# Modulation projections of a four-layer decoder step: eight single units in a row of weight units become bursts of four, and two of them move to another place in the plan

## The chip, the cores and the metric

The kernel runs on one NeuronCore of a Trainium2 chip. The metric is device time in microseconds (us) of one execution; the median of three runs before the change is 1632.8 us (1631.33 to 1634.27).

## What is computed

Four trunk layers run over 288 token rows at once: 256 rows of one prompt and 8 samples of 4 rows. Everything is fp32, with D = 1024. Each layer has two sub-layers, a token mixer and a squared-ReLU MLP, and each sub-layer is modulated per sequence (adaLN):

```
mod = silu(c) @ w_ada[i] + b_ada[i]            # 9 sequences, 1024 -> 6 x 1024
sh1, sc1, g1, sh2, sc2, g2 = split(mod, 6)
h = x * (1 + sc1) + sh1
x = layer_norm(ALPHA * x + g1 * mixer(h), ...)  # 0: gMLP, 1: HGRN2, 2: MLA, 3: gMLP
h = x * (1 + sc2) + sh2
x = layer_norm(ALPHA * x + g2 * (square(relu(h @ w1)) @ w2), ...)
```

The mixers are: layers 0 and 3 a chunked gating MLP (gMLP), layer 1 a gated linear recurrence with state (HGRN2), layer 2 a latent attention over a paged cache of 2048 positions (MLA). `w_ada` is a 1024 x 6144 matrix per layer, 24 MB, and it is read once for nine rows of input.

## The kernel before

Activations are kept transposed: features on partitions, the 288 rows along the free dimension. A weight matrix comes in **weight units** of 1 MB (1024 rows x 256 columns). A unit is loaded into a `raw` tile, split into a rounded high part (`hi`, ScalarE, L240) and the rest (`lo`, VectorE, L241), each in two pieces, and is then used in 16 positions of three matmuls each (`mm3`, L294, L295, L297: hi x hi, lo part x hi, hi x lo part), 48 matmuls of 128x128 by 288 columns. There are 5 `raw` tiles (`RAWB`) and 3 pairs of `hi` and `lo` (`HLB`), so at most three units are split ahead.

A **modulation unit** is 1 MB of `w_ada`, loaded into the same 5 `raw` tiles but used as it is, in fp32: `ada_step` (L492 on, its matmul is L504) issues four matmuls of 512 columns, one for each group of 32 output partitions, and the profile shows them as 8 instructions. An `ada` unit covers 128 rows of two of the six chunks (eight units make chunks 0 and 1, or 2 and 3); an `adh` unit covers 256 rows of one chunk (four units make chunk 4, the second scale, or chunk 5, the second gate). After the last unit of a chunk `ada_end` or `adh_end` copies the sums out, turns them with small matmuls (L539 or L525) and writes them to `modT`. A layer needs 8 + 8 + 4 + 4 units. There are 88 of them behind the first two chunks of layer 0, which have a form of their own (L558).

**The order of loads** is written out by hand: `run` makes one `plan`, a list of weight and modulation units, and `load_next` issues its loads in that order on SyncE's queue (L138 for modulation, L145 for weights). `advance` issues a load whenever fewer than five units from the first unfinished one on have been issued, splits a weight unit if a `hi`/`lo` pair is free (`pump`), and otherwise tries `ada_step`. So a modulation unit that isn't used yet holds one of the five tiles.

**When a modulation unit may be used** is set by `s.quota` (how many may go), `s.alim` (up to which unit of the plan), `s.hold`, and `s.fence` (an instruction that they stand behind on TensorE). `wfree` is called at the last matmul of each weight unit; it raises the quota by one and moves the fence to that matmul, so one modulation unit follows each weight unit. At each LayerNorm boundary (`run`) the quota is set to `FILL` = 4 and the fence to the last matmul of the statistics, so four units run in the LayerNorm, where TensorE waits for the normalized rows. `ada_need` forces all units up to a key, whatever the quota.

The framework (Tile) schedules instructions by priority in program order: an instruction may be placed on its engine ahead of earlier ones that aren't ready in the scheduler's model. On the chip each engine then keeps the order that the scheduler chose. `issue_after` fixes one instruction behind another.

In the plan before, `spread` puts four modulation units behind the first two weight units of a stage and then one behind each weight unit (mixers) or every second one (MLP). A mixer of layers 1 to 3 takes chunks 2 and 3 (eight units, four of which run in the LayerNorm ahead of it) and chunk 4; an MLP takes chunk 5 (in the LayerNorm ahead of it) and the next layer's chunks 0 and 1. `before_out` stands ahead of the mixer's output projection (four weight units, here called o0 to o3), `before_end` ahead of the MLP's last matrix. The output projection's first two units run interleaved over their eight k tiles, so that the k tiles that are ready first go first.

In the HGRN2 mixer four pairs of heads follow one another; the last pair's chain of small matmuls, VectorE and ScalarE steps has no weight units behind it but the output projection. In the MLA mixer the paged cache rows also go through the `raw` tiles, two per sample; the merge of the partial softmaxes and the value projection stand ahead of `before_out`.

Of the kernel before, what the change touches and what calls it, by code (L numbers as in the profile page):

```python
# [45 lines left out]
R2 = (1, 5)  # L46
# [3 lines left out]
AHEAD = 4  # L50

FILL = 4
SPACE = (1, 1, 1)

VEC = {}

# [1 line left out]
class Net:  # L58
# [42 lines left out]
    def set_plan(s, plan):  # L101
        s.plan = plan
        s.idx = {}
        w = 0
        s.wlist = []
        s.alist = []
        s.ndone = 0
        s.fence = None
        s.hold = True

        s.quota = 99
        s.alim = -1
        s.quiet = False
        s.rs_ins = s.rs_act = None
        for n, (kind, key, src) in enumerate(plan):
            assert key not in s.idx, key
            s.idx[key] = n
            if kind in ("w", "w2", "t", "q"):
                s.wlist.append(n)
            if kind == "a":  # L120
                s.alist.append(n)
        s.rawt = {}
        s.done = [False] * len(plan)
        s.nd = 0
        s.freed = 0
        s.nsplit = 0
        s.piece = 0
        s.wdone = 0
        s.hl = {}
# [132 lines left out]
    def wfree(s, key):  # L262
        assert s.wlist[s.wdone] == s.idx[key], (key, s.plan[s.wlist[s.wdone]][1])
        s.wdone += 1
        del s.hl[key]
        s.quota = max(s.quota, 0) + 1
        s.fence = s.last_mm
        s.advance()


# [1424 lines left out]
            out.append(u)  # L1695
        return out + a

    def spread(s, w, a, first, n, step):

        out, a = list(w[:first]) + list(a[:n]), list(a[n:])  # L1700
        for k, u in enumerate(w[first:]):
            out.append(u)
            if a and k % step == step - 1:
                out.append(a.pop(0))
        return out + a

    def before_out(s, i):
        if i != s.layers[0]:
            s.ada_need(("adh", i, 4, 3))
        s.hold = True  # L1710

    def before_end(s, i):
# [7 lines left out]
    def run(s):  # L1720
        L = s.layers
        af = s.ada_first_units(L[0])
        plan = []
        for n, i in enumerate(L):
            kind = i % 3
            a, o = getattr(s, ("plan_gmlp", "plan_hgrn", "plan_mla")[kind])(i)
            f = s.plan_ffn(i)
            first, last = n == 0, n + 1 == len(L)
            sc2, g2 = s.adh_units(i, 4), s.adh_units(i, 5)
            if first:  # L1730
                plan += af[:4] + a[:2] + af[4:] + s.merge(a[2:] + o, s.ada_units(i, 1) + sc2, *FIRST)
            else:
                plan += s.spread(a, s.ada_units(i, 1) + sc2, 2, FILL, SPACE[i % 3]) + o
            fill = g2 + ([] if last else s.ada_units(L[n + 1], 0))
            plan += s.spread(f[0] + f[1], fill, 2, FILL, 2) + f[2] + f[3]
        s.set_plan(plan)
        s.alim = s.idx[("adh", L[0], 4, 3)]
        s.setup()
        s.late_setup()
        for n, i in enumerate(L):  # L1740
            first, last = n == 0, n + 1 == len(L)
            s.hold = False
            s.alim = s.idx[("adh", i, 4, 3)]
            if n:
                s.quota = FILL
                s.advance()
            s.rs_ins = None
            getattr(s, ("gmlp", "hgrn", "mla")[i % 3])(i)
            if first:
                s.ada_need(("adh", i, 4, 3))  # L1750
            s.prep_ab(i, 1, s.lnv(0, i), s.lnv(1, i))
            if first:
                s.bias_means()
            s.boundary(1, i)
            s.fence = s.last_stat
            s.hold, s.quota = False, FILL
            s.alim = s.idx[("adh", i, 5, 3) if last else ("ada", L[n + 1], 0, 7)]
            s.advance()
            s.ada_need(("adh", i, 5, 3))
            s.quota = 0  # L1760
            s.rs_ins = None
            s.ffn(i)
            if not last:
                s.boundary(0, i)
                s.fence = s.last_stat
            else:
                s.store_y(i)
# [89 lines left out]
```

## Time and profile before

| | |
|---|---|
| median of three runs | 1632.8 us |
| the profiled execution's own time | 1632.95 us |
| its span (first to last instruction) | 1631.2 us |
| TensorE matmul busy | 1580.3 us, 97% |
| VectorE busy | 1026.6 us, 63% |
| ScalarE busy | 801.4 us, 49% |
| granted TensorE clock, mean | 0.989 of full speed |
| read from HBM | 324.09 MB, 203 GB/s over the span |

The profile is one execution. PE is TensorE's matmuls and PEld its weight loads, DVE is VectorE, ACT ScalarE, SP SyncE, whose queue issues the loads. An instruction's line is that of the kernel's source; tiles are named as `out<-in`. Matmuls are pipelined: two neighbours of 288 columns start 0.13 us apart though each lasts 0.29 us, so costs on TensorE are read from start to start.

### The profile page before, as it was taken

To read this page: it belongs to the slowest core of one execution; us is meant where nothing else is said; L and a number is where in the kernel's file an instruction comes from. 1 tells how busy PE (TensorE), PEld (TensorE's weight loads), DVE (VectorE), ACT (ScalarE), POOL (GpSimd) and SP (SyncE) were. 2 spreads that over 40 slices of the span, in tenths; PEclk is the share of its full clock that TensorE was granted. 3 is DMA by queue.
4 is the path that set the end of the run, shared out by engine and by line. 5 is a ranking of instruction groups with operands and counts; after the bars stand their busy time and mean duration, and the time that the engine had idled before them with its cause. 6 is when DMAs were issued, how large, how long until landed. Compare 5 with 4: busy or idle time off the path is not lost.

```text
span 1631.2 us, 30568 instructions
## 1 busy us (share of the span) xinstructions
PE 1580.3 (97%) x12538; PEld 1402.3 (86%) x12538; DVE 1026.6 (63%) x2290; ACT 801.4 (49%) x1437; POOL 53.2 (3%) x70
## 2 busy tenths in 40 slices
PE   7999999999999989999999999999999999999997
PEld 3878889998789878999977666878999888899997
DVE  3558745658768886556686335595455685874655
ACT  2554633545767755335353445364354463653542
POOL 1000000000110100000002120000000000000000
PEclk9998999999999999999999999899999999999999
DMA  9976876458764567755476445287654676655531
GB/s 323 340 254 209 297 239 181 157 179 269 230 190 158 158 200 273 245 166 170 157 256 248 143 151 207 95 278 261 217 174 158 236 263 200 207 182 170 166 104 43
DMA packets 222719, 332.61 MB, mean 204 GB/s; under 512 B 7171, under 2 KB 196041, under 8 KB 213362
## 3 DMA queue, kind: packets, MB, share of 16 engines
q1 hardware_dynamic: 215954, 299.86, 55.7%
q0 software_dynamic: 6624, 30.78, 5.6%
q8 instruction: 99, 1.62, 0.4%
q14 instruction: 42, 0.34, 0.1%
HBM read 324.09 MB, written 6.53 MB: 203 GB/s over the span
## 4 chain that ended last, share of the span: by engine, by line
PE 87%; DVE 6%; DMA 3%; ACT 2%; issue 1%; SPq 0%; POOL 0%; DVEq 0%; ACTq 0%; POOLq 0%
PE mm L294 23%; PE mm L297 22%; PE mm L295 22%; PE ada L504 4%; DMA raw<-in_w_ada 2%; PE mm L1456 1%; DVE lo L241 1%; PE mx L1474 1%; PE mm L1510 1%; PE mx L1528 1%; PE ada L558 1%; PE mx L863 1%; PE mx L965 1%; PE mx L1478 1%; PE mm L1556 1%
## 5 line engine op out<-in xcount | busy, mean ns | idle before, releaser
L241 DVE TENSOR_TENSOR lo<-raw,hi 128x1024 fp32r<-128x1024 f32 x360 | 434.4, 1222 | 172.1 <-ACT hi L240 172.0
L240 ACT ACTIVATE hi<-raw 128x1024 fp32r<-128x1024 f32 x360 | 371.0, 1052 | 262.1 <-PE mm L297 198.5
L294 PE MATMUL mm<-Hi,hi 128*128 128x288 f32 x1064 | 317.4, 302 | 7.6 <-ACT Hi L1209 4.5
L295 PE MATMUL mm<-Hi,lo 128*128 128x288 f32 x1064 | 314.4, 299 | 0.1
L297 PE MATMUL mm<-FL,hi 128*128 128x288 f32 x1024 | 303.6, 296 | 0.0
L294 PE MATMUL mm<-FH,hi 128*128 128x288 f32 x1024 | 303.3, 296 | 0.0
L295 PE MATMUL mm<-FH,lo 128*128 128x288 f32 x1024 | 299.2, 292 | 0.0
L297 PE MATMUL mm<-Lo,hi 128*128 128x288 f32 x1064 | 297.4, 298 | 0.0
L294 PEld LDWEIGHTS mm<-Hi,hi 128*128 128x128 f32 x1064 | 200.2, 188 | 36.2 <-issue 11.7
L294 PE MATMUL mm<-OH,hi 128*128 128x288 f32 x704 | 207.1, 298 | 1.4 <-ACT OH L705 1.3
L295 PEld LDWEIGHTS mm<-Hi,lo 128*128 128x128 f32 x1064 | 200.6, 189 | 7.2 <-issue 5.0
L295 PE MATMUL mm<-OH,lo 128*128 128x288 f32 x704 | 205.7, 296 | 0.5 <-DVE lo L241 0.5
L297 PEld LDWEIGHTS mm<-Lo,hi 128*128 128x128 f32 x1064 | 193.8, 189 | 8.6 <-issue 7.5
L295 PEld LDWEIGHTS mm<-FH,lo 128*128 128x128 f32 x1024 | 195.1, 191 | 2.5 <-issue 2.5
L294 PEld LDWEIGHTS mm<-FH,hi 128*128 128x128 f32 x1024 | 192.4, 188 | 5.0 <-issue 5.0
L297 PE MATMUL mm<-OL,hi 128*128 128x288 f32 x704 | 195.1, 296 | 0.0
L297 PEld LDWEIGHTS mm<-FL,hi 128*128 128x128 f32 x1024 | 191.9, 187 | 0.0
L784 ACT ACTIVATE r<-mm 128x288 f32<-128x288 f32 x128 | 52.3, 412 | 184.5 <-PE mm L297 179.0
L294 PEld LDWEIGHTS mm<-OH,hi 128*128 128x128 f32 x704 | 132.1, 188 | 11.9 <-issue 5.0
L295 PEld LDWEIGHTS mm<-OH,lo 128*128 128x128 f32 x704 | 132.4, 188 | 0.8 <-DVE lo L241 0.7
L297 PEld LDWEIGHTS mm<-OL,hi 128*128 128x128 f32 x704 | 128.0, 188 | 1.9 <-issue 1.7
L786 DVE TENSOR_TENSOR s<-r 128x288 f32<-128x288 f32 x128 | 58.2, 457 | 110.7 <-ACT r L784 110.7
(434 smaller groups left out, 2067.3 us busy)
## 6 DMA issues: line engine op xcount, KB each, us to landing
raw<-in_ffn_w SPq DMA_DIRECT2D x128, 1024.0 KB, 5.6
raw<-in_w_ada SPq DMA_DIRECT2D x88, 1024.0 KB, 5.5
raw<-in_a_w_in SPq DMA_DIRECT2D x16, 1024.0 KB, 7.3
raw<-in_b_w_in SPq DMA_DIRECT2D x16, 1024.0 KB, 6.6
raw<-in_w_ada SPq DMA_DIRECT2D x16, 512.0 KB, 9.8
raw<-in_a_w_out SPq DMA_DIRECT2D x8, 1024.0 KB, 6.6
St<-in_state_hgrn POOLq DMA_DIRECT2D x8, 512.0 KB, 5.6
out_hs_s<-St POOLq DMA_DIRECT2D x8, 512.0 KB, 3.8
```

The costliest lines, as they stand in the source:

```text
L240: nc.scalar.activation(hi[:, a:b], r[:, a:b], AF.Copy)
L241: nc.vector.tensor_tensor(lo[:, a:b], r[:, a:b], hi[:, a:b].bitcast(F32), op=OP.subtract)
L294: mm(out, w[0], x[0], start=first, stop=False)
L295: mm(out, w[1], x[0], start=False, stop=False)
L297: s.last_mm = mm(out, w[0], x[1], start=False, stop=last).ins
L504: nc.tensor.matmul(s.pa[32 * j:32 * j + 32, :], x, w, start=(k == 0), stop=(k == last), skip_group_check=True)
L558: mm = nc.tensor.matmul(pa[r0:r0 + 32, :], s.scT[:, 2 * kp + par, :], t[:, par, h, :], start=(kp == 0), stop=(kp == 3), skip_group_check=True)
L784: nc.scalar.activation(r, ps[:, :T], AF.Relu)
L786: nc.vector.tensor_tensor(sq, r, r, op=OP.mult)
L863: nc.tensor.matmul(pt[:, 128 * q:128 * q + 128], vt01[:, q, sl], s.wsT[:, c, :], start=True, stop=True)
L965: mm(pt[32 * b:32 * b + 32, 64 * hh + 32 * g:64 * hh + 32 * g + 32], k[:, hh, a:a + 32], q[:, hh, a:a + 32], start=True, stop=True, skip_g ...
L1456: tr(pt[:, 128 * n:128 * n + 128], lat[b][t // 8][:, t % 8, 128 * c:128 * c + 128], s.id)
```

## The change

A stage's modulation units outside the LayerNorms get their quota not after every weight unit but at two points, behind the stage's second and fourth weight unit (`wburst`), four at a time; the plan is reordered to it (`burst`). The mixer's limit `alim` ends with chunks 2 and 3, and chunks 4 and 5 (second scale, second gate) are planned among o0 to o3 and forced in `before_out`: both chunks in layers 1 and 2, there without a fence, chunk 4 alone in layer 3. So the MLPs of layers 1 and 2 no longer take chunk 5, and their LayerNorm runs the next layer's first four units in its place. In layer 0 the mixer's plan stays as it is, but its units get no fence; its MLP still takes chunk 5 in the LayerNorm and then has all eight units of the next layer outside it.

```diff
-SPACE = (1, 1, 1)
...
+        s.wburst = ()
...
         del s.hl[key]
-        s.quota = max(s.quota, 0) + 1
-        s.fence = s.last_mm
+        if s.wdone in s.wburst:
+            s.quota, s.fence = FILL, s.last_mm
         s.advance()
...
-    def spread(s, w, a, first, n, step):
...
+    def burst(s, w, a):
+        return list(w[:2]) + list(a[:FILL]) + list(w[2:3]) + list(a[FILL:]) + list(w[3:])

     def before_out(s, i):
         if i != s.layers[0]:
+            s.ada_need(("ada", i, 1, 7))
+            if i % 3:
+                s.fence = None
             s.ada_need(("adh", i, 4, 3))
+            if i != s.layers[-1]:
+                s.ada_need(("adh", i, 5, 3))
         s.hold = True
...
-                plan += s.spread(a, s.ada_units(i, 1) + sc2, 2, FILL, SPACE[i % 3]) + o
-            fill = g2 + ([] if last else s.ada_units(L[n + 1], 0))
-            plan += s.spread(f[0] + f[1], fill, 2, FILL, 2) + f[2] + f[3]
+                plan += s.burst(a, s.ada_units(i, 1)) + s.merge(o, sc2 + ([] if last else g2), *R2)
+            fill = (g2 if first or last else []) + ([] if last else s.ada_units(L[n + 1], 0))
+            plan += s.burst(f[0] + f[1], fill) + f[2] + f[3]
...
-            s.alim = s.idx[("adh", i, 4, 3)]
+            s.alim = s.idx[("ada", i, 1, 7) if n else ("adh", i, 4, 3)]
             if n:
                 s.quota = FILL
+                s.wburst = (s.wdone + 2, s.wdone + 4)
                 s.advance()
...
-            if first:
-                s.ada_need(("adh", i, 4, 3))
+            s.ada_need(("adh", i, 4, 3))
...
             s.alim = s.idx[("adh", i, 5, 3) if last else ("ada", L[n + 1], 0, 7)]
+            s.wburst = (s.wdone + 2, s.wdone + 4)
             s.advance()
             s.ada_need(("adh", i, 5, 3))
-            s.quota = 0
```

`R2` is (1, 5): `merge` puts o0 first, then five modulation units, then o1, then the rest, then o2 and o3.

## Rows read from the trace of the kernel before

**Rows 1.** The page: busy time by engine, shares of the chain that ended last

```profile
PE 1580.3 (97%) x12538; PEld 1402.3 (86%) x12538; DVE 1026.6 (63%) x2290; ACT 801.4 (49%) x1437; POOL 53.2 (3%) x70
...
PE 87%; DVE 6%; DMA 3%; ACT 2%; issue 1%; SPq 0%; POOL 0%; DVEq 0%; ACTq 0%; POOLq 0%
```

**Rows 2.** Windows, modulation matmuls alone: stretch, length, busy (count), clock, DMA share, GB/s

```profile
45.00:156.50 111.50, 13.82 (x96) 0.95 0.76 263
160.80:377.40 216.60, 8.53 (x64) 1.00 0.64 209
```

**Rows 3.** Timeline of PE around one single unit in layer 0's MLP

```profile
208.80 0.30 PE L294 MATMUL mm<-Hi,hi 128*128 128x288 f32 x1
208.94 0.29 PE L295 MATMUL mm<-Hi,lo 128*128 128x288 f32 x1
209.16 1.06 PE L504 MATMUL ada<-raw,scT 128*32 128x512 f32 x8
210.15 0.40 PE L297 MATMUL mm<-Lo,hi 128*128 128x288 f32 x1
210.39 0.29 PE L294 MATMUL mm<-Hi,hi 128*128 128x288 f32 x1
```

**Rows 4.** Timeline of PEld at the same place: the first weight load behind the unit

```profile
210.15 0.19 PEld L297 LDWEIGHTS mm<-Lo,hi 128*128 128x128 f32 x1 [0.84 <-issue]
```

**Rows 5.** Timeline of PE in the LayerNorm ahead of layer 0's MLP

```profile
156.57 3.64 PE L504 MATMUL ada<-raw,scT 128*32 128x512 f32 x32
160.84 0.40 PE L294 MATMUL mm<-Hi,hi 128*128 128x288 f32 x1 [0.63 <-ACT Hi L705]
```

**Rows 6.** Waits of PE over the whole span: waiter, releaser, us in total, times, longest

```profile
PE ada L504 <- DMA raw<-in_w_ada: 2.0, 4, 0.7
```

**Rows 7.** Issues on SP's queue around layer 0's first LayerNorm

```profile
153.15 4.91 SPq L145 DMA_DIRECT2D raw<-in_ffn_w  x2
158.55 0.35 SPq L138 DMA_DIRECT2D raw<-in_w_ada  x1
159.41 3.28 SPq L145 DMA_DIRECT2D raw<-in_ffn_w  x2
172.76 0.34 SPq L138 DMA_DIRECT2D raw<-in_w_ada  x1
```

**Rows 8.** Issue to landing (last number, us): the load at 160.27, the one at 172.76

```profile
raw<-in_ffn_w SPq DMA_DIRECT2D x1, 1024.0 KB, 13.2
...
raw<-in_w_ada SPq DMA_DIRECT2D x1, 1024.0 KB, 5.2
```

**Rows 9.** The page's costliest groups: the two halves of a split; busy, mean ns

```profile
L241 DVE TENSOR_TENSOR lo<-raw,hi 128x1024 fp32r<-128x1024 f32 x360 | 434.4, 1222 | 172.1 <-ACT hi L240 172.0
L240 ACT ACTIVATE hi<-raw 128x1024 fp32r<-128x1024 f32 x360 | 371.0, 1052 | 262.1 <-PE mm L297 198.5
```

**Rows 10.** Groups of PE by line: the small matmuls behind a chunk of four units

```profile
L525 PE MATMUL mx<-con,adas 128*128 128x18 f32 x64 | 8.7, 271 | 0.0
```

**Rows 11.** Windows, PE alone, ahead of the output projections of layers 1 and 2

```profile
570.50:575.00 4.50, 0.00 (x0) 1.00 0.72 209
575.00:579.00 4.00, 3.98 (x18) 0.57 0.00 0
1015.00:1025.00 10.00, 5.27 (x49) 1.00 0.96 299
1025.00:1036.60 11.60, 10.76 (x52) 0.56 0.20 78
```

**Rows 12.** Waits of PE from 548 to 580, the end of the HGRN2 mixer

```profile
PE mm L294 <- ACT Hi L1209: 4.5, 1, 4.5
PE mx L1038 <- DVE k L991: 1.3, 1, 1.3
PE mx L1030 <- DVE k L991: 0.9, 1, 0.9
```

**Rows 13.** Issues on SP's queue from 499 to 552, layer 1

```profile
532.55 13.55 SPq L145 DMA_DIRECT2D raw<-in_ffn_w  x2
```

More of the change, by code (lines that the diff above doesn't have):

```diff
@@ L1696, in merge @@
         return out + a
-    def spread(s, w, a, first, n, step):
[L1700 to L1705, printed above, removed]
+    def burst(s, w, a):
+        return list(w[:2]) + list(a[:FILL]) + list(w[2:3]) + list(a[FILL:]) + list(w[3:])
     def before_out(s, i):
         if i != s.layers[0]:
+            s.ada_need(("ada", i, 1, 7))
+            if i % 3:
+                s.fence = None
             s.ada_need(("adh", i, 4, 3))
+            if i != s.layers[-1]:
+                s.ada_need(("adh", i, 5, 3))
         s.hold = True
```

## The prediction

> **What bounds the kernel now.** The page first: PE is busy in 97% of the span and holds 87% of the chain that ended last [rows 1]. So a change is worth what it takes from PE's stream, or what it adds to it in waits. Next the windows cut at the LayerNorms, counting the modulation matmuls alone [rows 2]: 64 instructions, that is 8 units, stand outside the LayerNorms in layer 0's MLP and as many in five more stages (MLPs of layers 1 and 2, mixers of layers 1, 2, 3), and 96 in layer 0's mixer. Then what one costs. Around a single unit [rows 3] the matmul before it starts at 208.94 and the second one after it at 210.39, 1.45 us for what takes two steps of 0.133 (208.80 to 208.94 is one): **1.19 us for a single unit**. Four in a row last 3.64 us [rows 5] where one lasts 1.06, so each further unit adds (3.64 - 1.06)/3 = **0.86 us**. A burst of four costs 1.19 + 3 x 0.86 = 3.77, against 4.76 for four singles. The LayerNorm's four are free: after them PE still waits 0.63 us for the rows [rows 5].
>
> Where do the 0.33 us of a single unit go? The weight load of the first ordinary matmul behind it starts together with that matmul, at 210.15, after 0.84 us without any load [rows 4]. The Trainium skill ("TensorE: Matmul & The Clock Gate", section "Step-by-step: what each phase is for") says that PE pulls weight loads ahead of matmuls in flight. By that, a single unit would cost its own 0.86 and grouping nothing; the eight bursts below would give 8 us less, 1625.5 us in place of my 1617.5. The skill's "TensorEngine Tiling (Array Packing)", "Key Properties", says instead that a change of tiling mode drains the engine, and the 0.84 us agree with that. I go by the row.
>
> **The change, part by part** (against the profiled execution's own 1632.95 us; the median is 0.15 less, so one sum serves both).
>
> *MLPs of layers 1 and 2.* Before: 8 singles, 9.5 us. After: four of them are in the LayerNorm, in the place of the second gate, and four in one burst, 3.8. Saved 5.7 each. Their waits for loads go too: 2.0 us in four waits in the whole kernel [rows 6], all in the three MLPs, of which I count half here and half for layer 0. Is everything there in time? The plan has four units and one weight unit (f3) behind the split of f2. In layer 0 the load that waits for f2's split goes out at 172.76, 12 us after the first matmul (160.84 [rows 5, 7]), and lands 5.2 us later [rows 8]. Here that load is f3: it lands at 17, its first half is split 2.3 us later (1.05 + 1.22 [rows 9]), and it is wanted after two weight units (96 steps, 12.8), the burst (3.8) and f2 (6.4), at 23. Spare: 3.5 us. Nothing is added. **Saved 12.4.**
>
> *Mixers of layers 1 and 2, the first part.* Before: 8 singles outside the LayerNorm; after: one burst of four there, and the other four go to the next part. **Saved 11.4** for both.
>
> *Mixer of layer 3.* 8 singles become two bursts, the second ahead of the projection, behind an old fence. o0, its four units and o1 fit the five tiles, since o0 gives its tile back when it is split. **Saved 2.0.**
>
> *MLP of layer 0.* 8 singles become two bursts: 9.5 + 1.0 of the waits - 7.5 = 3.0 saved. But here the plan has all eight between f2 and f3. Four sit in tiles until the first burst at 173.9. Their tiles come free about 175.1, 175.9, 176.8 and 177.6, and three more modulation loads go out ahead of f3. In the trace the fourth of four loads issued within 2.6 us, the one at 160.27, landed 13.2 us after its issue [rows 7, 8]. So f3 lands at 190.8, its first half is split at 193.1, and f2 is done at 173.9 + 3.8 + 6.4 = 184.1: **a wait of 9.0 us**. Alone in the queue it would take 5.2, a wait of 1.0; I take the fourth-of-four, which is the same situation. A wait like that also has a price behind it. After the 4.5 us without matmuls at 570.5 the granted clock was 0.57 for 4.0 us, with 18 matmuls where full speed (2.4 GHz) would need 2.4 us [rows 11]: 1.6 us. So this stage **loses 7.6**. On PE the second burst and f4 stand behind f3's matmuls, on SP's queue the loads of f4 and on stand behind f3's. What is late next would be f4: its load can take f3's tile once f3 is split (195), and lands at 200.4, before the second burst ends at about 205. If it has to wait for a unit of that burst instead, it comes some 4 us late; I keep that for the range.
>
> *The eight units ahead of the projection, layers 1 and 2.* Eight units in about three groups are 8 x 0.86 + 3 x 0.33 = 7.9 us, and two chunk ends (8 small matmuls each, 8.7/8 = 1.1 [rows 10]) 2.2, together 10.1 of PE work; the 2.2 disappear elsewhere. What can hide it in layer 1: waits of 4.5, 1.3 and 0.9 us [rows 12], now partly covered by the projection's ready k tiles; and the slow 4.0 us behind them, worth 1.6 if the clock stays up [rows 11]. 10.1 - 2.2 - 6.7 - 1.6 is about 0. In layer 2, PE has 4.7 us idle from 1015 to 1025, then 11.6 us at a clock of 0.56 [rows 11], worth up to 5 at full speed, of which I count half: again about 0. Loads: in layer 1 the two loads behind the projection's four now go out from 532.6 to 546 [rows 13]; in the new plan o0 and five modulation units are first, so those five sit in the five tiles by about 551, while o1 and three more units wait for the first five to run. These have no fence, so the first time PE lacks ready work, about 549, they go; o1 then lands about 555. Bounds for a layer: 3 us gained if the waits swallow all and the clock holds; 8 lost (7.9) if nothing hides. I take **1.5 lost each**, nearer to full cover: a unit can hold up a small matmul of the chain by its 0.86, once or twice. On DVE and ACT the splits of o1 to o3 come later than now (2.3 us a half, in turn [rows 9]); the chain's own steps have priority over them.
>
> *Layer 0's mixer.* Same units in the same plan, without a fence; they ran as singles at the pace of their loads (DMA share 0.76 [rows 2]). Nothing, within 2 us either way.
>
> Sum: 12.4 + 11.4 + 2.0 - 7.6 - 3.0 = 15.2 saved; 1632.95 - 15.2 is 1617.8, 1617.6 against the median. I say **1617.5**.
>
> **The rivals.**
>
> *Everything hides* (1606): f3's load passes quickly and the tails swallow their units and hold the clock. For it: DMA share 0.20 from 1025 [rows 11]. Against it: the queue is in order. 6 of the 9 us back, and 2 x 3 us gained rather than 3 lost: 1632.8 - 27.
>
> *Grouping does not pay* (1625.5): the scheduler places ready ordinary matmuls between the units of a burst, or the drain is overlapped as above. Against it: all four-unit groups in LayerNorms stayed whole, but there nothing else was ready.
>
> *The projection's second weight unit comes late* (slower, 1645). It is loaded behind five modulation units that hold all tiles. If the scheduler leaves those until the last wait at 570.5, o1 and the last three units go out from 571.5 to 574, the last lands 13.2 us later, 587 in place of a start at 575, and the three units (2.6) stand ahead of the projection: some 15 us in layer 1 and likewise in layer 2. 18.2 saved without the tails, less 30: 12 slower. It decides if the first forced unit of layer 1 starts after about 562; in one layer alone it gives about 1630. For it: no wait on PE is long before 549. Against it: they have no fence, and PE already reached for projection work at 548.
>
> **How the numbers follow.** Forecast 0.62; everything hides 0.12; grouping does not pay 0.11; late unit in both layers 0.10, in one layer (about no change) 0.05. A measurement tells 0.2% (3.3 us) from no change. The first three lie below 1629.5: faster 0.85, same 0.05, slower 0.10. The range reaches down past the case in which all hides, by the 2 us of layer 0's mixer (1604), and up past the unpaid case and a second wait in layer 0, to 1631.
>
> **What would show it.** Right: L504 groups of 32 instructions outside the LayerNorms, lasting 3.6 us; one at about 173.9 followed by 48 matmuls and a wait of about 9 us for a load or split; in layers 1 and 2 about 40 fewer single-unit steps, and both MLP windows 6 us shorter; the 4.5 us gap of layer 1's end mostly filled. Wrong: groups broken up by other matmuls, waits of the first projection matmuls on `hi` or `lo`, or MLP windows of layers 1 and 2 that don't shrink.

## The result, and the profile after

The changed kernel takes 1614.75 us (median; 1609.68 to 1621.26) against 1632.64 of the kernel before on the same chip: a ratio of 0.9892, with a 95% interval of 0.9855 to 0.9930. That is 17.9 us less, where 15.2 were forecast. The profiled execution took 1613.43 us, its span is 1611.7, 19.5 less than before's. The head of the page (busy time, chain) against [rows 1]:

```profile
PE 1566.9 (97%) x12538; PEld 1399.0 (87%) x12538; DVE 1025.4 (64%) x2290; ACT 798.8 (50%) x1435; POOL 53.1 (3%) x70
...
PE 87%; DVE 6%; DMA 4%; ACT 2%; issue 1%; SPq 0%; POOL 0%; DVEq 0%; ACTq 0%; POOLq 0%
```

TensorE has the same number of instructions and is still the bound. Of the 19.5 us, 13.4 are busy time and the rest is idle time. Where they went is read from windows cut at the last matmul of each LayerNorm's statistics (L642). Columns: stretch, length, PE busy (count), granted clock, DMA share, GB/s. Before, in order: MLP 0 (of layer 0), mixer and MLP 1, mixer and MLP 2:

```profile
155.90:379.10 223.20, 221.60 (x1656) 1.00 0.65 210
379.10:596.00 216.90, 206.71 (x2229) 0.99 0.61 193
596.00:818.00 222.00, 220.97 (x1653) 1.00 0.65 213
818.00:1069.90 251.90, 241.30 (x2058) 0.98 0.53 183
1069.90:1292.60 222.70, 221.06 (x1653) 1.00 0.65 213
```

The kernel after, with mixer 0 as its first line:

```profile
93.40:151.90 58.50, 57.34 (x389) 0.97 0.65 214
151.90:380.70 228.80, 221.61 (x1656) 0.99 0.63 205
380.70:592.30 211.60, 207.37 (x2270) 1.00 0.66 218
592.30:807.80 215.50, 214.41 (x1614) 1.00 0.61 200
807.80:1060.20 252.40, 246.81 (x2098) 0.99 0.56 199
1060.20:1275.50 215.30, 214.36 (x1614) 1.00 0.62 201
```

All stages against before and the forecast's terms (lengths from the cuts themselves, which the windows round to 0.1 us; mixer 3 in two parts, about its inner LayerNorm):

| stage | before, us | after, us | difference | forecast |
|---|---|---|---|---|
| start and mixer 0 | 94.6 + 61.3 | 93.4 + 58.5 | -4.0 | 0 |
| MLP 0 | 223.1 | 228.8 | +5.7 | +7.6 |
| mixer 1 | 217.0 | 211.6 | -5.4 | -4.2 |
| MLP 1 | 222.0 | 215.5 | -6.5 | -6.2 |
| mixer 2 | 251.9 | 252.4 | +0.5 | -4.2 |
| MLP 2 | 222.7 | 215.3 | -7.4 | -6.2 |
| mixer 3 | 40.3 + 72.3 | 39.1 + 71.1 | -2.4 | -2.0 |
| MLP 3 and end | 226.0 | 226.0 | 0 | 0 |

Of the terms that were forecast every sign but one came, and mixer 2 gave nothing. Now one row group per mechanism. First, a burst in layer 0's MLP on PE's timeline (start, us, instruction):

```profile
170.46 0.29 PE L297 MATMUL mm<-Lo,hi 128*128 128x288 f32 x1
170.68 3.64 PE L504 MATMUL ada<-raw,scT 128*32 128x512 f32 x32
174.25 0.40 PE L294 MATMUL mm<-Hi,hi 128*128 128x288 f32 x1
174.49 0.29 PE L295 MATMUL mm<-Hi,lo 128*128 128x288 f32 x1
```

From 170.46 to 174.49 are 4.03 us for what takes two steps of 0.133: the burst costs 3.76, as worked out (3.77). Second, what follows it: waits of PE in layer 0's MLP (waiter, releaser, total, times, longest), SP's issues there, and windows of PE.

```profile
PE mm L294 <- ACT hi L240: 6.2, 1, 6.2
PE mm L295 <- DVE lo L241: 0.4, 1, 0.4
```

```profile
153.66 20.19 SPq L138 DMA_DIRECT2D raw<-in_w_ada  x8
174.38 28.57 SPq L145 DMA_DIRECT2D raw<-in_ffn_w  x6
```

```profile
180.00:185.00 5.00, 0.90 (x7) 0.97 0.82 291
185.00:190.00 5.00, 2.54 (x9) 0.50 0.01 2
190.00:195.00 5.00, 5.00 (x34) 0.85 0.70 210
```

Eight modulation loads stand ahead of f3 on the queue, f3 goes out at 174.38, and the `hi` of its first half is there at 187.0, 6.2 us after f2's matmuls are done. The granted clock falls to its lower level (0.50) in this wait and is up again at about 191. Third, the ends of the mixers of layers 1 and 2, from L1017 of the last pair of heads and from the last L1608 to the LayerNorm's first matmul L639. Before:

```profile
549.20:593.70 44.50, 36.80 (x271) 0.96 0.38 124
1030.90:1067.60 36.70, 34.89 (x243) 0.93 0.23 76
```

After:

```profile
540.90:590.00 49.10, 47.17 (x357) 1.00 0.78 276
1010.00:1057.90 47.90, 46.12 (x298) 0.93 0.66 235
```

In layer 1 PE's waits in this stretch fall from 7.7 us (length less busy) to 1.9, the wait of 4.5 [rows 12] to 1.0, and the clock stays up. In layer 2 nothing comes back: the stretch is 11.2 us longer.

### The profile page after: what moved, and what is told of

It is laid out like the page before. It is cut to its first block, busy times and chain, and to the rows that moved or that the text cites. A ratio compares the mean times of both kernels' runs of the same rounds, so it can differ in the third digit from the quotient of the medians.

```text
span 1611.7 us, 30562 instructions
## 1 busy us (share of the span) xinstructions
PE 1566.9 (97%) x12538; PEld 1399.0 (87%) x12538; DVE 1025.4 (64%) x2290; ACT 798.8 (50%) x1435; POOL 53.1 (3%) x70
## 4 chain that ended last, share of the span: by engine, by line
PE 87%; DVE 6%; DMA 4%; ACT 2%; issue 1%; SPq 0%; POOL 0%; DVEq 0%; ACTq 0%; POOLq 0%
PE mm L294 23%; PE mm L297 23%; PE mm L295 22%; PE ada L504 3%; PE mm L1456 2%; DMA raw<-in_ffn_w 1%; DVE lo L241 1%; PE mx L1474 1%; PE mm L1510 1%; DVE Z L674 1%; PE mx L1528 1%; DMA raw<-in_a_w_in 1%; PE mx L863 1%; PE mx L1478 1%; PE mx L965 1%
```

## The experiments

My theory was the forecast's, with three places where it had lost: f3's load behind modulation loads (layer 0's MLP), units in pieces (layer 2's end), and units that hold up a chain of small matmuls (layer 1's end). The rivals: the granted clock, or the loads, or that all the gain came from moving units and none from grouping them.

**The same kernel again.** No edit.

> The changed kernel itself, for a second profile and more times: how far stage lengths repeat. My theory of the three stages that lost (layer 0's MLP +5.7 us, the last part of layer 1's mixer +5.0, of layer 2's +11.2) ties them to the order of instructions: each of them repeats within 1.5 us, and the 2.8 us that layer 0's mixer gave (same instruction order in both kernels) do not belong to the change and may be gone. Rival: the granted clock falls at other moments from one execution to the next and makes these differences; then the last part of layer 2's mixer comes back by 3 us or more. Time 1610 to 1621.

Measured: 1613.93 us (1610.45 to 1617.76), ratio 0.9892. MLP 0 took 228.7, mixer 1 210.7, MLPs 215.4 and 215.5: they repeat within 1 us. Mixer 2 took 249.9 against 252.4, more apart than the 1.5 that I had allowed and just short of the 3 of the rival; the difference lies behind L1608, where the clock was up this time:

```profile
1009.60:1054.70 45.10, 43.30 (x297) 1.00 0.70 248
```

So 2.8 us of this stretch are the clock's and come and go. The order's part is not the other 8.4 alone: before's 36.7 us had a clock of 0.93 too, and at like clocks (47.9 at 0.93) the stretch is 11.2 longer. Mixer 0 took 58.5 again, but over the runs below, all with the same instruction order there as before and after the change, it took 57.0 to 61.4, and before's 61.3 lies inside. On these numbers the 4.0 us of the table's first line can't be put down to the change. In each of these executions the clock fell, or did not, behind waits of 1.2 us in all between 115 and 125 us: from 115 to 135 it was 0.74 in before, 0.91 after, 1.00 in the run with f3 ahead.

**f3 ahead of the last four units.** Layer 0's MLP alone is planned otherwise:

```diff
-        return list(w[:2]) + list(a[:FILL]) + list(w[2:3]) + list(a[FILL:]) + list(w[3:])
+        return list(w[:2]) + list(a[:FILL]) + list(w[2:3]) + list(a[FILL:2 * FILL]) + list(w[3:4]) + list(a[2 * FILL:]) + list(w[4:])
```

> Layer 0's MLP alone is planned otherwise: the weight unit f3 goes ahead of the last four of the eight modulation units. Theory (f3's load stands behind modulation loads): the 6.2 us wait for f3's high half is gone, the MLP of layer 0 takes 222 to 223.5 us instead of 228.8, the whole kernel about 6 us less (1608 to 1609 by the median of 1614.8). If another load then comes late (modulation units of the second burst, behind f3), the wait is smaller but not gone: 225 to 227. Rival (the wait is the clock's or the split engines', not the queue's): 228 to 229, no change.

Measured: 1606.71 us (1602.21 to 1609.1), ratio 0.9845 (0.9828 to 0.9861). The stage's window, and SP's queue around it:

```profile
151.10:371.20 220.10, 219.48 (x1655) 1.00 0.65 213
```

```profile
167.92 0.38 SPq L145 DMA_DIRECT2D raw<-in_ffn_w  x1
170.99 2.90 SPq L138 DMA_DIRECT2D raw<-in_w_ada  x4
177.33 23.14 SPq L145 DMA_DIRECT2D raw<-in_ffn_w  x7
```

f3 now goes out 3 us ahead of the four, at 167.92; no wait on PE is left in the stage behind the LayerNorm. It takes 220.1 us, 8.7 less, better than I had said: 6.6 of waits and 2.1 of the clock behind them. What is left against before's 223.1 is 3.0, the gain of grouping eight singles into two bursts (and losing their load waits), to the tenth what the forecast's term said.

**The second gate in one piece, layer 2.** Its four units go behind the value projection's last matmul:

```diff
             if i != s.layers[-1]:
+                if i % 3 == 2:
+                    s.fence = s.last_mm
                 s.ada_need(("adh", i, 5, 3))
```

> In layer 2 alone the second gate's four units are held behind the last matmul of the value projection, so that they run in one piece ahead of the output projection, instead of in pieces among the small matmuls. Theory A (switching between the two kinds of matmul costs: about 0.33 us per piece, and the eight units stand in about eleven pieces): the last part of layer 2's mixer (50.2 us from the end of the merge to the LayerNorm) loses 2 to 3 us. Theory B (the units' own work is simply not hidden, 8 x 0.86 us): no change within 1 us, or up to 1 us more, as the waits that they filled come back (those were 5.6 us before the change; at most 3 us more then). Whole kernel: A 1612, B 1615 to 1618.

Measured: 1615.54 us (1608.19 to 1616.46), ratio 0.9882: the whole kernel can't resolve it, since its clock fell in mixer 0 (61.4 us) and behind L1608. The stretch from L1608 to the LayerNorm:

```profile
1014.30:1058.00 43.70, 41.92 (x298) 0.92 0.73 257
```

It is 43.7 at a clock of 0.92 against 47.9 at 0.93 after: 4.2 us less, theory A, and more than its 2 to 3. Why more is read from PE's timeline. In the second run of the changed kernel, at full clock, a unit (8 instructions) stands in two pieces:

```profile
1013.24 0.29 PE L297 MATMUL mx<-vl,hi 128*128 128x288 f32 x1
1013.46 1.05 PE L504 MATMUL ada<-raw,scT 128*32 128x512 f32 x2
1014.44 0.40 PE L294 MATMUL mx<-vh,hi 128*128 128x288 f32 x1
1014.67 0.29 PE L295 MATMUL mx<-vh,lo 128*128 128x288 f32 x1
1014.90 1.06 PE L504 MATMUL ada<-raw,scT 128*32 128x512 f32 x6
1015.89 0.40 PE L294 MATMUL mm<-OH,hi 128*128 128x288 f32 x1
1016.12 0.29 PE L294 MATMUL mx<-vh,hi 128*128 128x288 f32 x1
```

With the gate in one piece:

```profile
1031.86 0.29 PE L297 MATMUL mx<-vl,hi 128*128 128x288 f32 x1
1032.09 3.64 PE L504 MATMUL ada<-raw,scT 128*32 128x512 f32 x32
1035.66 0.40 PE L294 MATMUL mm<-OH,hi 128*128 128x288 f32 x1
1035.89 0.30 PE L295 MATMUL mm<-OH,lo 128*128 128x288 f32 x1
```

The piece of two matmuls takes 0.98 us to the next start (1013.46 to 1014.44), the piece of six 0.99, and a whole unit of eight 0.99 [rows 3]. The column groups of a unit overlap (the second piece's first three instructions start within 0.02 us and last 0.62 each), so a unit cut in two is paid nearly twice, not only 0.33 more: 1.17 + 1.18 (read as the single unit's 1.19 was) instead of 0.86 inside a burst. The gate's four units stood in seven such pieces: 8.2 us, against 3.77 in one.

**The second gate left out**, layers 1 and 2:

```diff
...
-            if i != s.layers[-1]:
-                s.ada_need(("adh", i, 5, 3))
...
-                plan += s.burst(a, s.ada_units(i, 1)) + s.merge(o, sc2 + ([] if last else g2), *R2)
+                plan += s.burst(a, s.ada_units(i, 1)) + s.merge(o, sc2, *R2)
...
-            s.ada_need(("adh", i, 5, 3))
+            if first or last:
+                s.ada_need(("adh", i, 5, 3))
```

Layer 1's gate rows are set to ones; layer 2's keep what layer 0 left in the same tile.

> The second gate of layers 1 and 2 is left out (its eight modulation units in all, loads included; the gate rows are set to ones), so the last part of each of the two mixers has four units instead of eight. Theory (layer 1's tail hides most of its units in the waits, layer 2's hides few): layer 1's mixer 1 to 2 us shorter, layer 2's 5 to 6.5 us shorter (4 x 0.86 + six pieces x 0.33 + one chunk end 1.1), whole kernel 6 to 8.5 us less, 1606 to 1609. Rival 1 (units cost the same in both tails, their own work and no more): 3.4 to 4.5 us shorter in each. Rival 2 (the tails lost for the clock or for the loads, not for the units): less than 2 us in each.

Measured: 1610.36 us (1608.82 to 1612.66), ratio 0.9859. Mixer 2 took 246.7 us: 5.7 less than 252.4, whose clock also fell (the theory's 5 to 6.5), but only 3.2 less than 249.9, where it did not. Behind L1608, at a clock like the 0.93 of the changed kernel's profile, the pieces' price shows:

```profile
1016.40:1055.40 39.00, 37.19 (x257) 0.92 0.55 180
```

That is 8.9 less than 47.9, where the gate's seven pieces and its chunk end come to 8.2 + 1.1. Ahead of L1608, 3.2 came back: 1.5 in a wait for `PpT`, the rest about what a clock of 0.66 from 995 to 1000 costs. Mixer 1 took 212.4, 0.8 more than with the gate, where I had said 1 to 2 less: a miss. PE's wait and its windows at the end of layer 1:

```profile
PE mm L294 <- ACT Hi L1210: 5.1, 1, 5.1
```

```profile
567.40:572.50 5.10, 0.14 (x2) 0.95 0.52 149
572.50:579.00 6.50, 6.37 (x27) 0.51 0.00 0
```

Half of the units taken away shortens the chain from L1017 to the projection's last k tiles only from 31.9 to 29.6 us; PE then stands for 5.1 us, and its clock is at the lower level (0.51) for the 6.5 us behind. In layer 1 the gate is free. (The MLPs took 0.6 and 1.5 us more here; that stays open.)

**Grouping alone, by pairs.** The kernel before, with a quota of two at every second weight unit, counted from each stage's start (`wpar`):

```diff
...
-        s.quota = max(s.quota, 0) + 1
-        s.fence = s.last_mm
+        s.quota = max(s.quota, 0)
+        if s.quota > 50:
+            s.fence = s.last_mm
+        elif s.wdone % 2 == s.wpar:
+            s.quota, s.fence = s.quota + 2, s.last_mm
...
```

> The kernel before with one thing altered: a modulation unit no longer follows each weight unit, two of them follow every second one. Same plan of loads, nothing moved to another stage, no bursts of four. Theory (a unit costs 0.33 us for each group that it stands in, on top of 0.86): some 24 pairs are joined, 8 us less than before, 1623 to 1627. Rival (the weight loads are pulled ahead of running matmuls, so grouping is free, and all the gain of the change came from moving units): 1631 to 1635, no change.

Measured: 1623.91 us (1618.78 to 1625.37), ratio 0.9922 (0.9896 to 0.9947). The number fits the theory, but its arithmetic does not: only 10 whole pairs stand in the trace, all in the mixers of layers 1 to 3; in the MLPs the plan has two weight units between two modulation units, so all 24 singles stayed, and the MLPs took the same time within 0.8 us. The mixers of layers 1, 2 and 3 gave 3.8, 1.9 and -0.3 us (5.4 together is more than 10 x 0.33; units that had stood in pieces came together), and 4.4 us of the profiled run are mixer 0's clock. In mixer 3 the clock fell behind a wait for `wr` (0.98 over the stage, 1.00 before, some 2 us), which is about what its four pairs save. What the run does settle is the price of one pair:

```profile
392.38 0.29 PE L301 MATMUL mm<-Lo,hi 128*128 128x288 f32 x1
392.61 1.92 PE L508 MATMUL ada<-raw,scT 128*32 128x512 f32 x16
394.46 0.40 PE L298 MATMUL mm<-Hi,hi 128*128 128x288 f32 x1
394.70 0.30 PE L299 MATMUL mm<-Hi,lo 128*128 128x288 f32 x1
```

392.38 to 394.70 less two steps is 2.05 us, where two singles are 2 x 1.19 = 2.38: 0.33 saved. So grouping does pay.

**Bursts without the moved part.** f3 ahead in every MLP; the second scale in the mixer's bursts, the gate in the MLP's LayerNorm:

```diff
...
-            if i != s.layers[-1]:
-                s.ada_need(("adh", i, 5, 3))
...
-                plan += s.burst(a, s.ada_units(i, 1)) + s.merge(o, sc2 + ([] if last else g2), *R2)
-            fill = (g2 if first or last else []) + ([] if last else s.ada_units(L[n + 1], 0))
+                plan += s.burst(a, s.ada_units(i, 1) + sc2) + o
+            fill = g2 + ([] if last else s.ada_units(L[n + 1], 0))
...
```

> The change without its moved part: bursts of four everywhere, but the second scale stays among the mixer's units and the second gate in the MLP's LayerNorm, as before; f3 ahead of the last units in every MLP, as in the run with f3 ahead. Layers 1 and 2 are to be compared with before (mixer and MLP together 439.0 and 474.6 us) and with the run with f3 ahead (427.3 and 465.1). Theory (both parts pay: grouping 8 singles into two bursts saves 2 to 3 us a stage, moving four units from the MLP's front saves the rest): 433 to 435 and 469 to 471, whole kernel 1616 to 1620. Rival 1 (grouping is all, the moved units only change place): 427 and 465, as with f3 ahead, 1606. Rival 2 (moving is all): 439 and 474, 1624 to 1626. Layer 0's MLP 220 in any case.

Measured: 1614.21 us (1611.19 to 1615.8), ratio 0.9865. Layer 1 took 212.8 + 219.8 = 432.6 us, layer 2 246.9 + 219.6 = 466.5. Grouping alone thus gives 6.3 and 8.1 us, more than I had said; against the run with f3 ahead, moving adds 5.4 in layer 1 and only 1.4 in layer 2, where the moved units stand in pieces. Layer 1 is near the theory's 433 and speaks against both rivals; layer 2 lies below the theory and near rival 1: there grouping is nearly all. Part of what moving adds is the clock. Here it fell at layer 1's end (0.92 from L1017, behind the wait of 4.5) as it had before, and in mixer 2 (0.98); with f3 ahead it was 1.00 in both. Against the changed kernel's first profile, whose clock also fell in layer 2 (252.4 + 215.3 = 467.7), moving loses 1.2 us there, so its sign in layer 2 is open. Nor do the whole kernels tell the two apart (0.9865, 0.9835 to 0.9895, against 0.9845). Mixer 3 took 113.0 us (before 112.6, after 110.2) in spite of two whole bursts: its clock was 0.98, and 0.66 from 1281 to 1286, behind a wait for `wr`.

**All three cures.** f3 ahead; the gate in one piece in layer 2; and in layer 1 behind the chain's last small matmul, L1115, where it ran as 2 and 30 instructions:

```diff
...
             if i != s.layers[-1]:
+                s.fence = (None, s.last_sq, s.last_mm)[i % 3]
                 s.ada_need(("adh", i, 5, 3))
```

> Three cures at once, each in a stage of its own: f3 ahead in layer 0's MLP; in layer 2 the second gate in one piece behind the value projection; in layer 1 the second gate in one piece behind the last small matmul of the chain, where TensorE then waits 5 to 7 us for the high halves. Layer 0's MLP: 220 (as measured alone). Layer 2's mixer: 245.5 where the clock stays up, 248.6 where it falls as in the run with the gate in one piece. Layer 1's mixer, theory (units among the chain's small matmuls hold the chain up by their full cost, and only the last wait is free): the chain from L1017 to the first matmul of the projection's last k tiles takes 29.5 us as it did without the gate, instead of 31.2, the four units fill its last wait, the clock stays up, and the mixer takes 209.5 to 210.5 instead of 211.5. Rival (the chain is not held up by units, its length is DVE's and ACT's): 211 to 213. Whole kernel 1598 to 1603.

Measured: 1603.62 us (1601.66 to 1604.72), ratio 0.9809 (0.9782 to 0.9837). MLP 0 220.2 and mixer 2 246.0, as expected (its end 41.3 us at full clock against 45.1: 3.8 less). Mixer 1 missed: 212.9, in the rival's range. The chain up to the last L1115 fell to 22.6 us (from 24.9; before 20.0), but from there to the projection's last k tiles it took 10.4 us instead of 7.0 (before 5.9). VectorE's timeline shows why:

```profile
559.76 0.75 DVE L1124 SCALAR_TENSOR_TENSOR rl<-rl,rr 128x576 f32<-128x576 f32 x1
562.48 0.20 DVE L528 TENSOR_TENSOR modT<-mx,bT 128x36 f32<-128x36 f32 x1 [1.97 <-PE mx L525]
562.59 0.75 DVE L1125 SCALAR_TENSOR_TENSOR rr<-rl,rr 128x576 f32<-128x576 f32 x1
```

The copy of the gate's sums (L528) stands in VectorE's order between two steps of the chain, and waits 1.97 us for the small matmuls behind the four units, which I had just made later. L1125, ready since L1124, stands behind it. The Trainium skill ("TensorE: Matmul & The Clock Gate", section "Architectural detail: the array is 16× 32×32, not 1× 128×128") calls VectorE and ScalarE strictly first in, first out; these rows agree.

**The copies behind the chain**, and the three cures once more:

```diff
...
-        for h in range(2):
+        with s.tc.issue_after(s.late) if s.late else nullcontext():
+          for h in range(2):
             nc.vector.tensor_tensor(
...
+                s.late = s.last_P if i % 3 == 1 else None
                 s.ada_need(("adh", i, 5, 3))
+                s.late = None
```

> As the run with all three cures, and in layer 1 VectorE's two copies of the second gate's sums (L528) are put behind the last step of the chain's VectorE work (the products P). In that run the first copy stood in VectorE's order ahead of the chain's L1125 and waited 1.97 us for the small matmuls behind the gate's four units, and the chain with it: 10.4 us from the last L1115 to the projection's last k tiles, against 5.9 before the change. Theory (that wait is why layer 1 gained nothing there): the stretch falls to 8 to 8.6 us, TensorE's last wait of 2.4 us shrinks under 0.5, the half clock behind it (1.4 us) does not come, and layer 1's mixer takes 209.5 to 211 instead of 212.9. Rival (the four units and the splits of o1 to o3 fill the stretch in any case, the copy was only last in line): 212 to 213. Whole kernel 1600 to 1602 against 1603.6, and 1603 to 1604.

> The run with all three cures once more, for a comparison on the same chip and for how far its stages repeat: layer 1's mixer 212.9 and the wait of VectorE for the small matmuls about 2.0 us again if both come from the order of instructions (theory); 210.5 to 211.5 if that run was only a bad one (rival). 1602 to 1605.

Measured: 1604.7 us (1602.19 to 1605.73) with the copies behind, 1605.58 (1597.82 to 1613.35) without, ratios 0.9819 and 0.9827: the whole kernel can't tell them apart. The stage can. Mixer 1 took 210.8 with them, 212.9 and 214.2 without (there with the wait of 2.0 on L528 again, so the order makes it). With the copies behind, VectorE's chain and PE's last wait:

```profile
559.20 0.75 DVE L1126 SCALAR_TENSOR_TENSOR rl<-rl,rr 128x576 f32<-128x576 f32 x1
559.98 0.76 DVE L1127 SCALAR_TENSOR_TENSOR rr<-rl,rr 128x576 f32<-128x576 f32 x1
```

```profile
PE mm L295 <- ACT Hi L1211: 0.4, 1, 0.4
```

The two steps follow each other, 10.4 us become 8.4, the wait of 2.4 is 0.4 and the clock stays up. Still, this is within 1 us of the change's own 211.6: in layer 1 the units' place gave nothing in the end.

**The scale back in the row**, layers 1 and 2, on top of that:

```diff
...
-                plan += s.burst(a, s.ada_units(i, 1)) + s.merge(o, sc2 + ([] if last else g2), *R2)
+                if last:
+                    plan += s.burst(a, s.ada_units(i, 1)) + s.merge(o, sc2, *R2)
+                else:
+                    plan += s.burst(a, s.ada_units(i, 1) + sc2) + s.merge(o, g2, *R2)
...
-            s.alim = s.idx[("ada", i, 1, 7) if n else ("adh", i, 4, 3)]
+            s.alim = s.idx[("ada", i, 1, 7) if last else ("adh", i, 4, 3)]
```

> As the run with VectorE's copies behind the chain, but in layers 1 and 2 the second scale's four units go back from the place ahead of the projection into the mixer's own row of weight units, as a burst behind the fourth one (3.77 us and a chunk end there). Layer 1, theory (among the chain's small matmuls the units cost their full price, nothing hides them): the chain from L1017 to the last L1115 takes 20 us instead of 22.6, the mixer 210 to 212, against 210.7. Rival (there they are hidden): chain 22, mixer 214 to 215. Layer 2, theory (there the scale's units, in pieces, fill waits of some 4 us): 249.5 to 251.5 against 248.6, 247.7 and 246.0; rival (pieces cost more than the waits give): 245 to 246.5 at a clock that stays up.

Measured: 1606.53 us (1605.23 and 1607.82). Layer 1 missed: 213.7, near the rival. The chain took 22.0, not 20; the end from L1017 was 2.3 us shorter (48.2 to 45.9) and the rest 5.2 longer. So of the 4.9 us that four units and a chunk end cost in a row, only about 2.3 show among the chain's small matmuls: my theory that they cost their full price there falls, more than half is hidden. Layer 2: 250.4, as theory; there PE waits again for `W` (1.8 us; 1.9 in before, no such wait after), which the pieces had filled, and the stage's clock is 0.98, against 0.99 with the copies behind (248.6 us): most of the 1.8 us between the two.

## Why the prediction was right, point by point

**The price of grouping** held exactly: 1.19, 2.05 and 3.76 us for one, two and four units. The rival by which weight loads are pulled ahead and grouping does not pay fell with the pairs and with the bursts that move nothing. The Trainium skill ("TensorEngine Tiling (Array Packing)", section "Key Properties") says that a change of tiling mode drains the engine. These traces agree, with 0.33 us for each group.

**MLPs of layers 1 and 2**: 12.4 forecast, plus the two chunk ends of 1.1 that left them (put under the projection's part); 13.9 measured. f3 was in time, as worked out.

**MLP of layer 0**: the wait was there, 6.2 us, not 9.0. The step "lands 13.2 us after its issue, split 2.3 later" was mis-sized: it landed 11.5 after its issue, and PE began when `hi` alone was there, 1.1 later. 1.7 + 1.2 is the difference. The slow clock behind it cost 2.1 instead of 1.6, and with 0.4 more for `lo`, 6.6 + 2.1 - 3.0 is the 5.7 measured. The grouping term, 3.0, is confirmed by the run with f3 ahead. The feared lateness of f4 did not come.

**First part of the mixers**: 11.4 forecast and 2.2 of chunk ends. Layer 1 gave 9.9 us up to L1017 and layer 2 7.6 up to the last L1500 (1014.6 before, 996.8 after), instead of 6.8 each. The mis-sized step is "8 singles outside the LayerNorm" at 1.19: in layer 1 three of those eight had stood in two pieces each, and the eight cost about 12.4 us, not 9.5. In layer 2 one had stood in three pieces, and the eight cost about 11.9; that its stage gave less than these prices come to (9.2) stays open.

**The eight units ahead of the projection**: "1.5 lost each" (3.7 with the chunk ends). Layer 1's end grew by 4.6, near. Layer 2's, from the last L1500 to L639, grew by 8.1, and by 5.4 where the clock stayed up. The step that failed is "eight units in about three groups": they stood in twelve pieces. I had the rule (0.33 per group) but not that the scheduler would cut units themselves, nor that a cut unit is paid twice. The kernel before had shown the first: three of layer 1's fenced singles were cut. And of the slow clock that was counted as half a gain there, the kernel got its share only in some executions.

**Layer 0's mixer**, "nothing, within 2 us": 2.8, by the clock, and 1.2 in the start. These 4.0 us, which can't be put down to the change, and the smaller wait made up for layer 2's 4.7, so that the total came out 2.8 us from the forecast is in part luck: errors that cancel. The late weight unit did not occur: the first forced unit of layer 1 ran at 540.5, well ahead of 562, and no PE wait for `hi` of the projection's weights is in the trace.

## What to carry to other kernels

Keep matmuls that use the array in another shape together, and look in the trace whether they stayed so: a piece of two instructions cost as much as eight here. A fence behind the value projection's last matmul kept four units whole (layer 2); other fenced units were cut (2 and 30 in layer 1). Count, before moving work into a gap, the loads that it puts ahead of the next unit on the queue, and the steps on other engines that it brings: one copy that waits, in order, ahead of a chain's step cost 2 us. Where the whole kernel spreads by several us, judge by stages, and at the same granted clock.

The version with all three cures takes 0.9809 (0.9782 to 0.9837) and, repeated, 0.9827 (0.9796 to 0.9858) of the time before, by these ratios 11 to 14 us less than the change. Some 8 of it come with f3 ahead alone (0.9845, 0.9828 to 0.9861); the rest is not clear of the spread.

## What was not expected of the hardware

A piece of a modulation unit takes the same from two instructions to eight (0.98 to 0.99 us to the next start). And TensorE's granted clock falls, or does not, in the same place of the same instruction order from one execution to the next: mixer 0 took 57.0 to 61.4 us, and layer 2's end 45.1 or 47.9. Of what makes it fall no run here shows more.
